# Value products of three attention stages with v as the stationary operand, two heads on the array's column halves, and a softmax normalised ahead of its transposes

## The chip, the cores and the metric

The kernel runs on one NeuronCore of a Trainium2 chip. The metric is the device time of one execution in microseconds (us), from runs of the whole program. The engines that matter here are TensorE (PE: matmuls and, as a kind of matmul, 128x128 transposes; its weight loads are a row of their own, PEld), VectorE (DVE), ScalarE (ACT) and the DMA queues. A matmul has a stationary operand, which is loaded into the array as weights, and a moving one, which streams past it; the result lands in one of eight PSUM banks.

## The reference, cut to what matters

The program is a small transformer of two layers on 256 latent and 256 context tokens, followed by a second network of four blocks. Three of its mixers contain the attention that the change touches: neighbourhood attention (8 heads of 64, 256 latent queries over 256 latent and 256 context keys, and the context's own attention), window attention (8 query heads on 2 key heads, 256 queries over 512 keys, with a sink in the sum), and a dilated attention of the second network (8 heads, 256 queries, three causal key patterns side by side). Each of them is, per head:

```
s = q @ k.T * scale + bias or mask
p = exp(s - max(s)) / (sum(exp(s - max(s))) [+ exp(sink - max(s))])
o = p @ v
```

and the heads' outputs, merged, go through an output projection. A fourth, the differential attention, uses the same step order but is not touched.

## The kernel before

All large matmuls are f32 split into a high and a low part (three products each, `mm3`, lines 211 to 214); attention's own products are plain f32. Weights stream in by DMA, ACT makes the high part and DVE the low part (`halves`, lines 258 to 266), and PE multiplies them in blocks (`block`, line 404).

Attention runs as a side stream. A `Side` (line 75) holds generators, and at the middle and the end of every projection block `tick` lets them take some steps (rate 0.6 to 1.5 steps a tick), so that attention's instructions are written between the projection's. Within an engine the build's scheduler then orders instructions by that order and by what is ready in its own model; on the chip every engine takes its queue in order.

`attend` (lines 628 to 643) is the step order of one group of units. A unit is one head and one query tile of 128 rows. In step i the scores of units i and i+1 are issued as a pair (the two heads sit on the array's row halves, lines 634 to 637), unit i gets its maximum (DVE) and exponential (ACT, with the row's sum), unit i-2 is transposed (`transposed`, lines 645 to 651: PE transposes into a bank `pT`, ACT copies it to `pTs`), and unit i-3 takes its value products (`pv`). There the transposed probabilities are the stationary operand and v moves, 64 columns of one head:

```
for j in range(4):
    net.mm(o, u.pT[:, j], u.g.v[:, j, u.h * 64:(u.h + 1) * 64], j == 0, j == 3)
```

So the output `o` (PSUM tile `oat`, in window attention `oc`) has tokens on partitions. When a group's units are through, DVE takes the reciprocal of the sums (`rden`, `crd`) and multiplies the output out of PSUM (`yna`, `yc`), PE transposes it to features on partitions (`ynt`, `yct`), and ACT and DVE split it into the operand of the output projection.

- Neighbourhood attention: classes `Lat` and `Ctx` (lines 784 to 834) and `Group.run` (lines 852 to 878), four groups f of four `Lat` units and two `Ctx` units (each `Ctx` unit covers both query tiles of the context). Beside it run the projections, the gated convolutions (`gcu`) and a second side stream, modulation sums on DVE (`aacc`, line 566).
- Window attention: class `Swa` and `swa_run` (lines 1205 to 1257), two query tiles of eight heads; heads h and h+4 are a pair. Beside it run the projections of the differential attention.
- Dilated attention: `Unit` and `Group` (lines 2073 to 2137), four groups of two heads; units with the second query tile have six key tiles, those with the first have three. The last group's steps run in `att.drain()` (line 2167), after the last projection.

## Time and profile before

| | |
|---|---|
| median of 3 runs | 2496.32 us (2495.28 to 2497.0) |
| the profiled execution: its own time / its span | 2498.09 us / 2496.3 us |
| granted TensorE clock, mean | 0.984 of full |
| busy: PE, PEld, DVE, ACT | 95%, 79%, 73%, 52% of the span |
| HBM | 181 GB/s over the span |

The span is the time from the first to the last instruction; the execution's own time also has what lies around it. Busy times are unions of an engine's records. Matmuls are pipelined, so their records overlap and a start-to-start distance tells more than a duration.

### The profile page before, as it was taken

How to read it: one execution, taken by the hardware profiler on the slowest of the kernel's cores; microseconds unless marked ns; L12 is line 12 of the kernel's file. 1: busy time of each engine (PE TensorE's matmuls, PEld its weight loads, DVE VectorE, ACT ScalarE, POOL GpSimd, SP SyncE). 2: the span in 40 equal slices, each digit the busy share in tenths (PEclk: the TensorE clock that was granted, in tenths of full speed). 3: DMA queues.
4: the chain of work that ended last, by engine and by line, in shares of the span. 5: the costliest groups of instructions: out<-in, count | busy, mean ns of one | idle time of the engine just before them, and what ended most of it. 6: DMA issues, size and time to landing. Idle time of an engine off the chain costs nothing.

```text
span 2496.3 us, 32333 instructions
## 1 busy us (share of the span) xinstructions
PE 2383.6 (95%) x11882; PEld 1981.9 (79%) x11882; DVE 1812.5 (73%) x3515; ACT 1299.0 (52%) x2230; POOL 13.0 (1%) x27
## 2 busy tenths in 40 slices
PE   7999999999899879999999999989999999999998
PEld 5878888888788658787877887877788788898886
DVE  5798988676686778989988556998744754646644
ACT  4445333232454568777776445775644544655533
POOL 0000000000000000000000000000000000000000
PEclk9999999999998999999999999999999999999999
DMA  8344455654221159999997654333665555554561
GB/s 275 115 133 163 152 186 190 215 163 166 75 81 56 55 170 321 331 324 338 313 352 264 194 189 144 102 102 126 220 199 172 186 185 167 146 153 136 191 196 51
DMA packets 381471, 455.15 MB, mean 182 GB/s; under 512 B 16680, under 2 KB 313337, under 8 KB 381305
## 3 DMA queue, kind: packets, MB, share of 16 engines
q1 hardware_dynamic: 375481, 445.86, 55.1%
q10 hardware_dynamic: 5824, 7.15, 0.9%
q8 instruction: 95, 1.56, 0.3%
q14 instruction: 71, 0.58, 0.1%
HBM read 451.91 MB, written 1.05 MB: 181 GB/s over the span
## 4 chain that ended last, share of the span: by engine, by line
PE 51%; DVE 7%; ACT 2%; DMA 2%; issue 1%; DVEq 0%; SPq 0%; ACTq 0%
PE gu L206 26%; PE acc L206 13%; PE pj L206 6%; DVE wl L226 3%; DMA wxr<-in_moe_w_dram 1%; DVE hcv L1730 1%; PE ht L209 1%; PE cvq L206 1%; PE po L206 1%; ACT wh L225 1%; PE oat L206 1%; DVE wxl L226 0%; PE mgp L206 0%; DVE c L1861 0%; PE pT L209 0%
## 5 line engine op out<-in xcount | busy, mean ns | idle before, releaser
L226 DVE TENSOR_TENSOR wl<-wr,wh 128x1024 fp32r<-128x1024 f32 (+1 forms) x510 | 590.9, 1186 | 168.7 <-ACT wh L225 167.7
L225 ACT ACTIVATE wh<-wr 128x1024 fp32r<-128x1024 f32 (+1 forms) x510 | 503.3, 1025 | 284.2 <-PE gu L206 55.9
L226 DVE TENSOR_TENSOR wl<-wxr,wh 128x1024 fp32r<-128x1024 f32 (+1 forms) x122 | 144.2, 1207 | 49.6 <-ACT wh L225 44.9
L566 DVE SCALAR_TENSOR_TENSOR aacc<-wr,sc,aacc 128x512 f32<-128x512 f32 x224 | 162.0, 761 | 14.6 <-DMA wr<-in_ada_w_dram 13.6
L206 PE MATMUL gu<-wh,xh 128*128 128x512 f32 x416 | 163.8, 394 | 2.6 <-ACT xh L229 2.6
L206 PE MATMUL gu<-wh,xl 128*128 128x512 f32 x416 | 162.9, 392 | 0.7 <-DVE xl L230 0.7
L206 PE MATMUL gu<-wl,xh 128*128 128x512 f32 x416 | 162.5, 391 | 0.0
L206 PE MATMUL gu<-wl,mgh 128*128 128x512 f32 (+1 forms) x384 | 146.3, 381 | 8.1 <-DVE wl L226 8.1
L225 ACT ACTIVATE wh<-wxr 128x1024 fp32r<-128x1024 f32 (+1 forms) x122 | 123.7, 1043 | 54.2 <-PE acc L206 13.9
L206 PE MATMUL gu<-wh,mgh 128*128 128x512 f32 (+1 forms) x384 | 144.9, 377 | 1.3 <-ACT wh L225 1.2
L226 DVE TENSOR_TENSOR wxl<-wr,wxh 128x1024 fp32r<-128x1024 f32 (+1 forms) x94 | 110.0, 1182 | 46.8 <-ACT wxh L225 43.7
L206 PE MATMUL gu<-wh,mgl 128*128 128x512 f32 (+1 forms) x384 | 143.1, 373 | 0.6 <-DVE mgl L226 0.6
L206 PE MATMUL acc<-wh,hid 128*128 128x512 f32 x416 | 135.3, 396 | 0.0
L435 ACT ACTIVATE sg<-gu,ry 128x256 f32<-128x256 f32 x88 | 41.2, 472 | 164.0 <-PE gu L206 158.8
L225 ACT ACTIVATE wxh<-wr 128x1024 fp32r<-128x1024 f32 (+1 forms) x94 | 95.0, 1024 | 43.4 <-PE acc L206 20.2
L436 DVE SCALAR_TENSOR_TENSOR sg<-gu,ry,sg 128x256 f32<-128x256 f32 x88 | 42.0, 480 | 103.8 <-ACT sg L435 103.8
L206 PE MATMUL acc<-wh,hh 128*128 128x512 f32 x352 | 115.9, 399 | 1.1 <-ACT wh L225 1.1
L206 PE MATMUL gu<-wxh,xh 128*128 128x512 f32 x288 | 113.6, 395 | 1.7 <-ACT xh L229 1.6
L206 PE MATMUL gu<-wxh,xl 128*128 128x512 f32 x288 | 113.2, 393 | 1.4 <-DVE ri L286 0.8
L206 PE MATMUL gu<-wxl,xh 128*128 128x512 f32 x288 | 113.0, 392 | 0.0
L206 PE MATMUL pj<-wh,xh 128*128 128x512 f32 (+1 forms) x248 | 96.9, 392 | 0.6 <-ACT xh L229 0.6
L206 PEld LDWEIGHTS gu<-wh,xh 128*128 128x128 f32 x416 | 78.3, 188 | 20.5 <-ACT xh L229 4.7
(548 smaller groups left out, 5847.0 us busy)
## 6 DMA issues: line engine op xcount, KB each, us to landing
wr<-in_ffn_w_dram SPq DMA_DIRECT2D x176, 512.0 KB
wr<-in_moe_w_dram SPq DMA_DIRECT2D x124, 512.0 KB
wr<-in_ffn_w_dram SPq DMA_DIRECT2D x45, 1024.0 KB
wr<-in_ada_w_dram SPq DMA_DIRECT2D x42, 1024.0 KB
wr<-in_moe_w_dram SPq DMA_DIRECT2D x28, 1024.0 KB
wxr<-in_ffn_w_dram SPq DMA_DIRECT2D x44, 512.0 KB
wxr<-in_moe_w_dram SPq DMA_DIRECT2D x40, 512.0 KB
wr<-in_attn_w_qkv_dram SPq DMA_DIRECT2D x54, 256.0 KB
```

The costliest lines, as they stand in the source:

```text
L206: self.nc.tensor.matmul(out, lhsT, rhs, start=start, stop=stop)
L209: self.nc.tensor.transpose(out, in_, self.ident)
L225: self.nc.scalar.activation(h, src, AF.Copy)
L226: self.split_op = self.nc.vector.tensor_sub(l, src, h.bitcast(F32))
L435: nc.scalar.activation(g, p[:, 0:n], AF.Silu, scale=rs[tt])
L436: nc.vector.scalar_tensor_tensor(g, p[:, n:2 * n], rs[tt], g, op0=OP.mult, op1=OP.mult)
L566: self.nc.vector.scalar_tensor_tensor(a[:, s], w, col, a[:, s], op0=OP.mult, op1=OP.add)
L1730: V.scalar_tensor_tensor(a, xx[:, j:j + 256], tap(j), a, op0=OP.mult, op1=OP.add)
```

## The change

The value products swap their operands: v, 64 columns of one head, becomes the stationary operand and the transposed probabilities move, 128 columns. The output has features on partitions: head h lands on PSUM partitions 64h to 64h+63 (in window attention the key head decides, h // 4), so two heads fill the two column halves of the array and their products are issued in turns, as a pair, in the step of the odd unit (`pvs`). The output is then split straight out of PSUM; the multiplication by the reciprocal and the transposes of the output are gone, and the deferred step that held them (`att.post`) too. Since rows of the output are now features, the normalisation cannot be done there: each unit divides its exponentials by their sum ahead of its transposes (`norm` and `normed`, one step after the exponential), by a reciprocal on DVE and a scaling in place, on ACT in neighbourhood attention and on DVE in the other two. In window attention the output's features come in another order, and the rows of `od_w_out` are permuted on the host to match.

```diff
--- before.py
+++ after.py
@@ attend
                 units[i].s()
+            if 0 < i <= n and hasattr(units[i - 1], "pvs"):
+                units[i - 1].norm()
             if 0 <= i - lag < n:
                 units[i - lag].t()
-            if 0 <= i - lag - 1 < n:
-                units[i - lag - 1].pv()
+            j = i - lag - 1
+            if 0 <= j < n:
+                if not hasattr(units[j], "pvs"):
+                    units[j].pv()
+                elif j % 2:
+                    for ab in zip(units[j - 1].pvs(), units[j].pvs()):
+                        for f in ab:
+                            f()
             yield
+
+    def normed(self, e, den, n=1, act=False):
+
+        rd = self.sm(n, "rd")
+        self.nc.vector.reciprocal(rd, den)
+        w = e.shape[1] // n
+        for j in range(n):
+            x, r = e[:, j * w:(j + 1) * w], rd[:, j:j + 1]
+            if act:
+                self.copy(x, x, r)
+            else:
+                self.nc.vector.tensor_scalar(x, x, r, None, op0=OP.mult)
 
     def transposed(self, e, nkt):
         p = self.ps([128, nkt, 128], "pT")
@@ -798,15 +820,19 @@
                                        OP.add, OP.max, mx[:, 1:2])
                 V.tensor_scalar(mx[:, 1:2], mx[:, 1:2], -1.0, None, op0=OP.mult)
                 u.e = net.t2([128, 512], "pe")
-                nc.scalar.activation(u.e, s, AF.Exp, bias=mx[:, 1:2], accum_out=u.g.den[:, u.qt, u.h:u.h + 1])
+                u.den = net.sm(1, "den")
+                nc.scalar.activation(u.e, s, AF.Exp, bias=mx[:, 1:2], accum_out=u.den)
+
+            def norm(u):
+                net.normed(u.e, u.den, act=True)
 
             def t(u):
                 u.pT = net.transposed(u.e, 4)
 
-            def pv(u):
-                o = u.g.out()[:, u.qt, u.h]
-                for j in range(4):
-                    net.mm(o, u.pT[:, j], u.g.v[:, j, u.h * 64:(u.h + 1) * 64], j == 0, j == 3)
+            def pvs(u):
+                hs = slice(64 * u.h, 64 * u.h + 64)
+                o = u.g.out()[hs, u.qt * 128:(u.qt + 1) * 128]
+                return [lambda j=j: net.mm(o, u.g.v[:, j, hs], u.pT[:, j], j == 0, j == 3) for j in range(4)]
 
         class Ctx(Lat):
             def mms(u):
@@ -823,15 +849,18 @@
                 mx = net.sm(2, "mx")
                 V.tensor_reduce(mx, s, AX.X, OP.max, negate=True)
                 u.e = net.t2([128, 512], "pe")
+                u.den = net.sm(2, "den")
                 for j in range(2):
                     nc.scalar.activation(u.e[:, j * 256:(j + 1) * 256], s[:, j], AF.Exp, bias=mx[:, j:j + 1],
-                                         accum_out=u.g.den[:, 2 + j, u.h:u.h + 1])
-
-            def pv(u):
-                for j in range(2):
-                    o = u.g.out()[:, 2 + j, u.h]
-                    for i in range(2):
-                        net.mm(o, u.pT[:, 2 * j + i], u.g.v[:, 2 + i, u.h * 64:(u.h + 1) * 64], i == 0, i == 1)
+                                         accum_out=u.den[:, j:j + 1])
+
+            def norm(u):
+                net.normed(u.e, u.den, 2, act=True)
+
+            def pvs(u):
+                hs = slice(64 * u.h, 64 * u.h + 64)
+                return [lambda j=j, i=i: net.mm(u.g.out()[hs, (2 + j) * 128:(3 + j) * 128], u.g.v[:, 2 + i, hs],
+                                                u.pT[:, 2 * j + i], i == 0, i == 1) for j in range(2) for i in range(2)]
 
         vall = self.a8([128, 4, 512], F32, "v")
 
@@ -846,13 +875,12 @@
 
             def out(g):
                 if g.o is None:
-                    g.o = net.ps([128, 4, 2, 64], "oat")
+                    g.o = net.ps([128, 512], "oat")
                 return g.o
 
             def run(g):
                 f = g.f
                 g.bias = net.t4([128, 2, 2, 256], "bias")
-                g.den = net.sm(8, "den").rearrange("p (a b) -> p a b", a=4)
                 for qt in range(2):
                     for i in range(2):
                         rq = qt * 2 + i
@@ -863,18 +891,7 @@
                 nc.gpsimd.tensor_add(b, b, cmask.to_broadcast([128, 16, 64]))
                 units = [Lat(g, h, qt) for qt in range(2) for h in range(2)] + [Ctx(g, h, 2) for h in range(2)]
                 yield from net.attend(units)
-                rd = net.sm(8, "rden")
-                V.reciprocal(rd, g.den.rearrange("p a b -> p (a b)"))
-                y = net.t2([128, 8, 64], "yna")
-                V.tensor_mul(y, g.o.rearrange("p a h d -> p (a h) d"), rd[:, :, None].to_broadcast([128, 8, 64]))
-
-                def turn():
-                    tp = net.ps([128, 4, 128], "ynt")
-                    for qt in range(4):
-                        net.tr(tp[:, qt], y[:, 2 * qt:2 * qt + 2, :])
-                    net.split(yT[1][0][:, f], yT[1][1][:, f], tp.rearrange("p a b -> p (a b)"))
-
-                att.post(2, turn)
+                net.split(yT[1][0][:, f], yT[1][1][:, f], g.o)
                 yield
 
         for f in range(4):
@@ -1225,13 +1242,15 @@
                 nc.scalar.activation(mx[:, 2:3], sink[:, h:h + 1], AF.Exp, bias=mx[:, 0:1])
                 V.tensor_add(u.den[:, h:h + 1], u.den[:, h:h + 1], mx[:, 2:3])
 
+            def norm(u):
+                net.normed(u.e, u.den[:, u.h:u.h + 1])
+
             def t(u):
                 u.pT = net.transposed(u.e, 4)
 
-            def pv(u):
-                g = u.h // 4
-                for j in range(4):
-                    net.mm(u.o[0][:, u.h], u.pT[:, j], cv[:, j, g * 64:(g + 1) * 64], j == 0, j == 3)
+            def pvs(u):
+                gs = slice(64 * (u.h // 4), 64 * (u.h // 4) + 64)
+                return [lambda j=j: net.mm(u.o[0][gs, u.h % 4], cv[:, j, gs], u.pT[:, j], j == 0, j == 3) for j in range(4)]
 
         def swa_run(qt):
             qs = slice(qt * 128, qt * 128 + 128)
@@ -1239,21 +1258,10 @@
             us = [Swa(o, den, h + 4 * i, qt) for h in range(4) for i in range(2)]
             for i, _ in enumerate(self.attend(us)):
                 if i == 1:
-                    o[0] = self.ps([128, 8, 64], "oc")
+                    o[0] = self.ps([128, 4, 128], "oc")
                 yield
-            rd = self.sm(8, "crd")
-            V.reciprocal(rd, den)
-            y = self.t2([128, 8, 64], "yc")
-            V.tensor_mul(y, o[0], rd[:, :, None].to_broadcast([128, 8, 64]))
-
-            def turn():
-                tp = self.ps([128, 4, 128], "yct")
-                for f in range(4):
-                    self.tr(tp[:, f], y[:, 2 * f:2 * f + 2])
-                self.split(yT[0][:, 0:4, qs], yT[1][:, 0:4, qs], tp)
-                self.ready.add(("swa", qt))
-
-            att.post(2, turn)
+            self.split(yT[0][:, 0:4, qs], yT[1][:, 0:4, qs], o[0])
+            self.ready.add(("swa", qt))
             yield
 
         class Diff:
@@ -2097,18 +2105,21 @@
                     c = slice(gs[0] * n, (gs[-1] + 1) * n)
                     V.scalar_tensor_tensor(e[:, c], dl[:, off + c.start:off + c.stop], slope, s, op0=OP.mult, op1=OP.add)
                 V.tensor_reduce(mx, e[:, 0:3 * n], AX.X, OP.max, negate=True)
-                nc.scalar.activation(e[:, 0:3 * n], e[:, 0:3 * n], AF.Exp, bias=mx, accum_out=g.den[:, 2 * qt + h:2 * qt + h + 1])
+                u.den = net.sm(1, "den")
+                nc.scalar.activation(e[:, 0:3 * n], e[:, 0:3 * n], AF.Exp, bias=mx, accum_out=u.den)
+
+            def norm(u):
+                net.normed(u.e[:, 0:384 * (u.qt + 1)], u.den)
 
             def t(u):
                 nt = 3 * (u.qt + 1)
                 u.pT = [net.transposed(u.e[:, j * 128:min(j + 4, nt) * 128], min(4, nt - j)) for j in range(0, nt, 4)]
 
-            def pv(u):
-                g, h, qt = u.g, u.h, u.qt
-                nt = 3 * (qt + 1)
-                for j in range(nt):
-                    b, kt = j // (qt + 1), j % (qt + 1)
-                    net.mm(g.out()[:, qt, h], u.pT[j // 4][:, j % 4], g.v[:, kt, b, h * 64:(h + 1) * 64], j == 0, j == nt - 1)
+            def pvs(u):
+                g, qt = u.g, u.qt
+                nt, hs = 3 * (qt + 1), slice(64 * u.h, 64 * u.h + 64)
+                return [lambda j=j: net.mm(g.out()[hs, qt * 128:(qt + 1) * 128], g.v[:, j % (qt + 1), j // (qt + 1), hs],
+                                           u.pT[j // 4][:, j % 4], j == 0, j == nt - 1) for j in range(nt)]
 
         class Group:
             def __init__(g, f):
@@ -2119,21 +2130,12 @@
 
             def out(g):
                 if g.o is None:
-                    g.o = net.ps([128, 2, 2, 64], "oat")
+                    g.o = net.ps([128, 256], "oat")
                 return g.o
 
             def run(g):
-                g.den = net.sm(4, "den")
                 yield from net.attend([Unit(g, h, qt) for qt in (1, 0) for h in range(2)])
-                rd = net.sm(4, "rden")
-                V.reciprocal(rd, g.den)
-                y = net.t2([128, 4, 64], "yna")
-                V.tensor_mul(y, g.o.rearrange("p a h d -> p (a h) d"), rd[:, :, None].to_broadcast([128, 4, 64]))
-                yield
-                tp = net.ps([128, 256], "ynt")
-                for qt in range(2):
-                    net.tr(tp[:, qt * 128:(qt + 1) * 128], y[:, 2 * qt:2 * qt + 2, :])
-                net.split(yT[0][:, g.f], yT[1][:, g.f], tp)
+                net.split(yT[0][:, g.f], yT[1][:, g.f], g.o)
                 yield
 
         att = Side(1.2)
@@ -2219,7 +2221,11 @@
     rel = np.clip(col[None, :] - col[:, None] + 15, 0, 30)
     consts["k_rpb"] = np.asarray(inputs["ev_rpb"])[0][:, 4:11][:, :, rel].transpose(0, 2, 1, 3)
     for name in [n for n in _INS if n != "ev_rpb"] + list(consts):
-        a = np.ascontiguousarray(inputs[name] if name in inputs else consts[name])
+        a = inputs[name] if name in inputs else consts[name]
+        if name == "od_w_out":
+            a = np.array(a)
+            a[0, 0:512] = a[0, 0:512].reshape(2, 4, 64, 1024).transpose(1, 0, 2, 3).reshape(512, 1024)
+        a = np.ascontiguousarray(a)
         arrays[f"in_{name}_dram"] = a
         args[name] = nc.dram_tensor(f"in_{name}_dram", a.shape, mybir.dt.from_np(a.dtype), kind="ExternalInput").ap()
     out = nc.dram_tensor("out_0_dram", (1, 256, 1024), F32, kind="ExternalOutput").ap()
```

## Rows read from the trace of the kernel before

**Rows 1.** Page: busy time, share of the span, instructions of each engine.

```profile
PE 2383.6 (95%) x11882; PEld 1981.9 (79%) x11882; DVE 1812.5 (73%) x3515; ACT 1299.0 (52%) x2230; POOL 13.0 (1%) x27
```

**Rows 2.** Stretches: length, busy PE, PEld, DVE, ACT, POOL; clock; DMA.

```profile
96.00:285.00 189.00, 186.53 (x1068) 158.78 (x1067) 166.65 (x375) 78.88 (x178) 5.20 (x2) 1.00 0.48 151
713.00:802.00 89.00, 85.73 (x518) 72.84 (x518) 56.68 (x247) 40.63 (x108) 0.00 (x0) 0.90 0.16 51
2165.00:2287.00 122.00, 118.50 (x800) 112.69 (x799) 65.19 (x91) 71.68 (x132) 0.00 (x0) 0.99 0.50 154
2273.00:2287.00 14.00, 10.63 (x84) 9.68 (x83) 9.42 (x15) 8.77 (x19) 0.00 (x0) 0.88 0.51 174
```

**Rows 3.** Tile pTs, its matmuls: count, ns min/median/max, first and last start, form.

```profile
L206 PE MATMUL oat<-v,pTs x192: 217/275/323, 99.8 to 230.8; 128*128 128x64 f32 x192
...
L206 PE MATMUL oat<-dvv,pTs x144: 217/275/421, 2178.8 to 2285.6; 128*128 128x64 f32 x144
...
L206 PE MATMUL oc<-swa,pTs x128: 218/275/422, 724.5 to 792.7; 128*128 128x64 f32 x128
```

**Rows 4.** Timeline of PE around one unit's value products: start, us, instruction, count.

```profile
99.60 0.33 PE L206 MATMUL pj<-wl,a_1h 128*128 128x384 f32 x1
99.77 1.00 PE L206 MATMUL oat<-v,pTs 128*128 128x64 f32 x8
100.58 0.42 PE L206 MATMUL pj<-wh,a_1l 128*128 128x384 f32 x1
100.84 0.33 PE L206 MATMUL pj<-wh,a_1h 128*128 128x384 f32 x1
```

**Rows 5.** Timeline of PE and its weight loads: matmuls on 32-column tiles.

```profile
25.62 0.15 PEld L206 LDWEIGHTS ada<-adw,scw 128*32 128x32 f32 x6 [0.17 <-issue]
25.63 1.06 PE L206 MATMUL ada<-adw,scw 128*32 128x512 f32 x6
```

**Rows 6.** Timeline of PE around two bursts of paired scores, dilated attention.

```profile
2168.35 0.34 PE L206 MATMUL pj<-wxh,xl 128*128 128x384 f32 x1
2168.62 1.57 PE L206 MATMUL S<-dqk 64*128 64x256 f32 x12
2170.11 0.45 PE L206 MATMUL pj<-wxh,xh 128*128 128x384 f32 x1
2170.40 0.34 PE L206 MATMUL pj<-wxl,xh 128*128 128x384 f32 x1
...
2174.50 0.94 PE L206 MATMUL S<-dqk 64*128 64x128 f32 x12
2175.37 0.88 PE L209 MATMUL pT<-cm,de 128*128 128x128 f32 x6
2176.00 0.42 PE L206 MATMUL pj<-wxh,xh 128*128 128x384 f32 x1
```

**Rows 7.** Tile yna: the multiplications of the output out of PSUM.

```profile
L869 DVE TENSOR_TENSOR yna<-oat,rden x4: 691/692/692, 127.5 to 231.1; 128x512 f32<-128x512 f32 x4
L2131 DVE TENSOR_TENSOR yna<-oat,rden x4: 423/424/425, 2188.8 to 2286.0; 128x256 f32<-128x256 f32 x4
```

**Rows 8.** Groups of DVE, differential attention: busy us, mean ns | idle before.

```profile
L1277 DVE TENSOR_SCALAR pe<-pe,drd 128x512 f32<-128x512 f32 x8 | 3.9, 483 | 0.2
...
L1275 DVE RECIPROCAL drd<-dden 128x2 f32<-128x2 f32 x8 | 1.3, 160 | 2.2 <-ACT pe L1272 2.1
```

**Rows 9.** Groups of ACT: a copy with one scale per partition.

```profile
L222 ACT ACTIVATE dvv<-pj,ry 128x384 f32<-128x384 f32 x8 | 4.3, 574 | 3.1 <-PE pj L206 3.1
```

**Rows 10.** Waits of ACT, 96 to 242 us: total, times, longest.

```profile
ACT pe L801 <- DVE mx L799: 20.0, 11, 6.3
```

**Rows 11.** Timeline of PE, window attention: scores of a pair, then of single heads.

```profile
720.38 1.13 PE L206 MATMUL S<-swa 64*128 64x512 f32 x4
...
747.80 1.12 PE L206 MATMUL S<-swa 64*128 64x512 f32 x2
...
750.78 1.12 PE L206 MATMUL S<-swa 64*128 64x512 f32 x2
```

**Rows 12.** The stretch from 771 to 787 us, columns as in rows 2.

```profile
771.00:787.00 16.00, 14.47 (x70) 12.94 (x69) 7.84 (x46) 5.26 (x15) 0.00 (x0) 0.57 0.10 38
```

## Prediction

> **What bounds the kernel now.** I read the page first: PE is busy 95% of the span and DVE 73% [rows 1]. A matmul's record overlaps the next one's, so this share alone proves little; the second view is the busy time by stage, over the three stretches in which the changed code runs [rows 2]. Neighbourhood attention and the projection behind it (96 to 285 us) have PE busy 186.53 of 189.00 us, and DVE 166.65. Window attention (713 to 802) has PE 85.73 of 89.00, DVE 56.68. Dilated attention (2165 to 2287) has PE 118.50 of 122.00, DVE 65.19, ACT 71.68. So in all three the matmul queue is the nearest bound: a PE step saved is time saved, as long as the engine that feeds it keeps up. In the third stage that is easy, in the second likely, in the first doubtful: DVE is idle there only 189.0 - 166.7 = 22.3 us. The one stretch where PE really stands still is the tail of the dilated stage, after its last projection (2273 to 2287, PE 10.63 of 14.00 us): there the attention chain itself sets the end.
>
> **Value products.** Today one unit (a head and a query tile) issues 4, 6 or 3 f32 products. The trace has two MATMULs for each: 192 + 144 + 128 = 464 of them, every one behind a weight load of 128 columns, with only 64 columns moving [rows 3]. A unit of four runs from 99.77 to 100.58, 0.81 us for 8 MATMULs, and the matmul behind it takes 0.26 instead of 0.17 to hand over [rows 4]: 0.90 us a unit, 1.80 a pair, 0.1125 a MATMUL. A pair of units with six products is 24 x 0.1125 = 2.70, with three 1.35.
>
> Afterwards v stands still (64 columns of weights) and 128 columns of probabilities move, two heads on two column halves. The trace has no 128x64 tile, so I bound it by its two nearest rows. Column tiles do run side by side: six MATMULs on 32-column tiles with 512 columns moving, two rounds of three (of four in the code; a record can be missing), take 1.06 us in all [rows 5]. And two heads on row halves with exactly 128 columns moving run 12 MATMULs, six rounds, from 2174.50 to 2175.37, 0.87 us [rows 6]. Against the same burst with 256 columns (2168.62 to 2170.11, 1.49) the difference is 0.62 / 6 = 0.103 us a round; 0.87 - 6 x 0.103 = 0.25 is the cost of changing the array's mode at the start, and the matmul after the long burst needs 0.29 instead of 0.17. With 0.27 instead of 0.17 ahead of the burst that makes some 0.45 a burst for loads of 128 columns. By 0.103 us per 128 columns the two rounds of 512 on column tiles are 0.82, six in turn would be 2.5; a last record reaches 0.19 beyond its successor's start (1.00 against 0.81, [rows 4]), so of the 1.06 next to nothing is left inside, and for 32 columns I put 0.2 for entry and exit. For 64 columns I take 0.38, nearer to the burst of scores, whose rounds are the same. A pair of four products is then 8 x 0.103 + 0.38 = 1.20 us (1.02 to 1.27) against 1.80; of six 1.62 against 2.70; of three 1.00 against 1.35.
>
> Sum on PE: 12 pairs in the first stage and 8 in the second, 20 x 0.60 = 12.0; 4 x (1.08 + 0.35) = 5.7 in the third. **Transposes of the output** go: 16 + 8 + 8, at 0.63 / 6 = 0.105 each [rows 6], 3.4. Together 21.1 us of PE: 8.9 in the first stage, 5.6 in the second, 6.6 in the third.
>
> **Normalisation.** What goes: ten multiplications out of PSUM, 0.69 us or 0.42 [rows 7], and ten reciprocals. What comes, once a unit, 56 times, between the exponential and the transposes: a reciprocal on DVE (0.16) and a scaling (0.48 for 512 columns on DVE, [rows 8]). In the first stage the scaling is ACT's: 24 units, 16 of 512 columns and 8 of two times 256. A copy of 384 columns with a scale per partition takes 0.574 [rows 9], stretched to 512 columns 0.77, to 256 0.38: 16 x 0.77 + 16 x 0.38 = 18.4 us more on ACT, which works 78.88 of the 189.00 us there. DVE there: 24 x 0.16 - 4 x (0.69 + 0.16) = +0.4, nothing. In the second, DVE: 16 x (0.16 + 0.48) - 2 x 0.85 = +8.5 on 56.7 of 89; in the third 8 x (0.16 + 0.72) + 8 x (0.16 + 0.36) - 4 x 0.58 = +9.0 on 65.2 of 122 (0.72 and 0.36 are 0.483 stretched to 768 and 384 columns). None of that fills an engine; what counts is its place. The unit's transposes now wait for one more step. What hides it is that a unit's transposes come two steps of the planner after its scores, with projection matmuls in between; without that cover it costs 0.65 to 0.9 us a unit. The first stage's scaling also queues in ACT, where the weight splits and the copies of transposed probabilities stand behind it, and its reciprocal queues behind DVE's modulation sums: there ACT already waits 20.0 us, 11 times, for DVE's maxima [rows 10].
>
> **What of it reaches the end.** First stage: 8.9, but DVE keeps its load, and PE cannot run ahead of the weight splits; I take 60%, 5.3 (0 if DVE becomes the bound, 8.9 if not). Second: 60% of 5.6, 3.4, since PE is not full there now and DVE gets 8.5 more. Third: three of four groups lie under projections, 3 x 1.64 = 4.9, of which 4.3. The fourth is bare: its chain loses the multiplication and two transposes (0.42 + 0.21) and 1.4 of value products, and gains the hop of 0.9 at its start and DVE's queue for the next units; I call it 0, between -1.5 and +1.5. Against this: the two heads of a pair must be ready together. For the scores, which are paired already, it mostly holds, but in the second stage two of eight pairs came apart: one head alone needs 1.12 us for its two MATMULs, where both heads need 1.13 for four [rows 11]. A value pair that comes apart costs 1.20 more than one that holds (a second burst with its mode change). Four of 28 would cost 4.8, of which 3.3 on the path. Sum: 5.3 + 3.4 + 4.3 + 0 - 3.3 = 9.7 us.
>
> **The clock** is a term without a sign. From 771 to 787 us the granted clock is 0.57 of full [rows 12], that is mostly the lower of the two levels, 1.2 GHz, with PE busy 14.47 of 16 us. It costs some 16 x 0.43 = 6.9 us. If the new bursts do without it, that much comes on top; a second such episode takes as much. I take 0 and keep both ends.
>
> **A page that speaks against it.** In the row on column tiles the second round's weight loads are out 0.15 us after the first's, while the first round still runs, and all of it ends after 1.06 [rows 5]. The Trainium skill, TensorE: Matmul & The Clock Gate, section Part 3: Packing small matmuls (The mechanism), says that a weight load overlaps matmuls in flight only where their row groups differ; two column halves share all rows. By that rule the next loads would stand bare between the rounds, which is rival 1 and its time. The row contradicts it, for 32 columns.
>
> **Rivals.** (1) Loads bare between the rounds: 20 x 8 + 4 x 12 + 4 x 6 = 232 rounds, each with some 0.09 (what stands ahead of a burst of scores for its first loads, [rows 6]): 21 us, all of the gain, 2496. Against it: [rows 5]. (2) Pairs come apart for the most part, because the odd head's copy arrives later than the even one's: with half of them 16.8 of the 21.1 are gone and the time is 2496; with all 28, 20 x 1.20 + 4 x 1.62 + 4 x 1.00 = 34.5, net 13 slower, 2510. (3) The other side: **the normalising hop sits on the path of the transposes**. Place: ACT's queue in the first stage (behind a reciprocal that waits in DVE's), DVE's in the other two. Price: PE waits up to 0.65 to 0.9 us in a unit that no projection fills. It decides from 13.0 / 56 = 0.23 us a unit on, the gain on the path ahead of what pairs lose; at 0.9 in half the units, 25 us, the time is 12 higher, 2508. For it: [rows 10], and PE takes its queue in order. Against it: PE is full in these stretches because other matmuls fill such waits already. (4) DVE becomes the bound in the first stage and the second gives half: 4.3 + 1.7 - 1.5 = 4.5, 2492. (5) All of it reaches the end, 21.1, and the clock's 6.9: 2468.
>
> **How the numbers follow.** The profiled execution has a span of 2496.3 and its own time is 2498.1; the median of the runs is 2496.3, 0.07% lower, so the sum is taken off the median: 2496.3 - 9.7 = 2486.6. Chances: forecast (2478 to 2492) 0.60; rival 1 0.04; rival 2 0.10; rival 3 0.12; rival 4 0.10; rival 5 0.04. The range reaches to 2473 below and 2500 above; outside lie most of rivals 3 and 5 and the worst of 2. A measurement of this kernel tells some 0.2%, 5 us, from no change. Faster by more: 0.57 of the forecast, rival 5, half of 4 and a little of 2, 0.70. Within: the rest of these, rival 1 and half of rival 2, 0.16. Slower: rival 3 and the worst of 2, 0.14.
>
> **What the profile after would show.** Value products with the form 128x64 tiles and 128 columns moving, two at a time, 16 in about 1.0 us: the pair holds; bursts of 8 at 0.11 each: it came apart. The matmuls after a burst handing over in 0.29: the mode change. PE waiting for the scaled probabilities ahead of the transposes by more than a few us in a stage: rival 3. The stage from 96 to 285 as long as before with DVE at 95%: rival 4. The tail from 2273 to 2287 longer or shorter than 13.7 us tells the bare chain. The forecast is wrong above all if the weight splits on DVE, not PE, set the pace of the first stage, or if the planner's new order opens a gap that drops the clock elsewhere.

## The result, and the profile after

The changed kernel is slower: 2511.17 us median (2509.77 to 2514.74, four runs) against 2496.03 (2495.28 to 2497.0, four runs of before beside them). The ratio is 1.0052, with an interval of 1.0036 to 1.0068. The prediction said 2486.6, within 2473 to 2500, so both its sign and its range were wrong. The profiled execution has a span of 2508.0.

The first view is the page's busy time of after, whole span:

```profile
PE 2372.8 (95%) x11850; PEld 1958.4 (78%) x11850; DVE 1825.5 (73%) x3583; ACT 1316.7 (53%) x2262; POOL 12.9 (1%) x27
```

PE is busy 10.8 us less than in [rows 1] and the program takes 11.7 us longer. So PE stands still for longer. The 10.8 is about half of the 21.1 that the prediction takes away; part of the rest hides in matmuls that take longer at a lower clock (the run without the division, below, has PE busy 2367.7 us, 15.9 less than before, at a mean granted clock of 0.983). Where PE stands still is in the windows. The stages now lie elsewhere in time, so I cut them at their own ends, rounded to whole us: neighbourhood attention from its first transposed probabilities to the last `gcu` product, dilated attention from its first scores to the output projection (118.0 us before and 122.0 after, unrounded). First before, then after (window, its length, busy time and number of records of each engine, granted clock, DMA share, GB/s):

```profile
95.00:240.00 145.00, 142.53 (x869) 122.47 (x867) 125.00 (x289) 66.03 (x154) 5.20 (x2) 1.00 0.46 146
2169.00:2287.00 118.00, 114.50 (x778) 108.97 (x775) 62.35 (x88) 68.20 (x127) 0.00 (x0) 0.99 0.51 156
```

```profile
95.00:251.00 156.00, 140.59 (x851) 113.33 (x851) 129.52 (x315) 82.64 (x187) 5.04 (x2) 0.96 0.44 135
2176.00:2297.00 121.00, 111.91 (x754) 102.38 (x752) 67.99 (x112) 68.05 (x125) 0.00 (x0) 0.96 0.48 143
```

The neighbourhood stage went from 145 to 156 us. PE's idle time in it rose from 145.00 - 142.53 = 2.5 to 156.00 - 140.59 = 15.4, and the granted clock fell from 1.00 to 0.96. DVE has 129.52 of 156 us: it is not the bound. What PE waits for is in the view of waits. Each line names who waited, for what, us in total, how often, the longest. After, 90 to 252 us, and then 2157 to 2298:

```profile
PE pT L209 <- ACT pe L222: 15.4, 7, 4.0
...
PE pT L209 <- DVE rd L658: 8.5, 3, 4.7
PE pT L209 <- DVE de L665: 0.6, 1, 0.6
```

In the same two stretches before, PE waited ahead of `pT` for 0.4 and for 2.9 us. So what PE idles in the first stage is nearly all transposes that wait for the scaling on ACT, and 9.1 us in the third are transposes that wait for the scaling on DVE (the view names the reciprocal where that one ended last; in the longest of these waits, the unit's scaling ends at 2291.90 us, within 0.1 us of the reciprocal named). This is the prediction's rival 3.

One such wait in full, after, from the timeline (start, length, engine, line, operation, tiles; in brackets the idle time before it and what ended it):

```profile
143.35 0.96 PE L206 MATMUL S<-qk 64*128 64x512 f32 x6
...
144.54 0.69 ACT L824 ACTIVATE pe<-S,mx 128x512 f32<-128x512 f32 x1 [1.94 <-DVE mx L821]
145.07 0.41 DVE L818 TENSOR_REDUCE mx<-S 128x1 f32<-128x256 f32 x1
...
145.40 0.48 DVE L564 TENSOR_SCALAR aacc<-wr,sc 128x512 f32<-128x512 f32 x1
145.80 0.48 DVE L819 CUSTOM_DVE_ANT_0 S<-S,bias,mx 128x256 f32<-128x256 f32 x1
...
146.20 0.48 DVE L564 TENSOR_SCALAR aacc<-wr,sc 128x512 f32<-128x512 f32 x1
146.60 0.14 DVE L821 TENSOR_SCALAR mx<-mx 128x1 f32<-128x1 f32 x1
146.66 0.74 DVE L566 SCALAR_TENSOR_TENSOR aacc<-wr,sc,aacc 128x512 f32<-128x512 f32 x1
146.84 0.69 ACT L824 ACTIVATE pe<-S,mx 128x512 f32<-128x512 f32 x1 [1.03 <-DVE mx L821]
147.32 0.15 DVE L658 RECIPROCAL rd<-den 128x1 f32<-128x1 f32 x1
...
147.52 0.71 ACT L222 ACTIVATE pe<-pe,rd 128x512 f32<-128x512 f32 x1
...
148.29 0.48 PE L209 MATMUL pT<-cm,pe 128*128 128x128 f32 x1 [3.98 <-ACT pe L222]
```

The unit's exponential ends at 145.23. Its reciprocal, 0.15 us of work, starts at 147.32: ahead of it in DVE's queue stand the next unit's maximum (four instructions between 145.07 and 146.74) and three instructions of the modulation sums (0.48, 0.48 and 0.74 us), one behind the other with no idle time. Its scaling starts at 147.52: ahead of it in ACT's queue stands the next unit's exponential, which itself waits 1.03 us for that maximum. The hop is 0.15 + 0.71 us of work and takes 3.0 us. PE has nothing else in its queue that it may do first and stands still for 3.98 us.

The value products came out as priced. After, timeline of PE, a pair of four products and, from the dilated tail, a pair of six:

```profile
107.91 1.09 PE L206 MATMUL oat<-pTs,v 128*64 128x128 f32 x16
108.93 0.66 PE L209 MATMUL qkt<-cm,qkn 128*128 128x128 f32 x4
...
2295.16 1.53 PE L206 MATMUL oat<-pTs,dvv 128*64 128x128 f32 x24
2296.62 0.55 PE L209 MATMUL pT<-cm,de 128*128 128x128 f32 x3
```

From the burst's start to the next instruction it is 1.02 us for four products of two heads and 1.46 for six.

### The profile page after: what moved, and what is told of

It reads as the page before. It is cut to its first block, busy times and chain, and to the rows that moved or that the text cites. A ratio compares the mean times of both kernels' runs of the same rounds, so it can differ in the third digit from the quotient of the medians.

```text
span 2508.0 us, 32382 instructions
## 1 busy us (share of the span) xinstructions
PE 2372.8 (95%) x11850; PEld 1958.4 (78%) x11850; DVE 1825.5 (73%) x3583; ACT 1316.7 (53%) x2262; POOL 12.9 (1%) x27
## 4 chain that ended last, share of the span: by engine, by line
PE 50%; DVE 8%; ACT 2%; DMA 1%; issue 1%; SPq 0%; DVEq 0%; ACTq 0%
PE gu L206 26%; PE acc L206 13%; PE pj L206 5%; DVE wl L226 3%; DVE hcv L1738 1%; PE ht L209 1%; PE po L206 1%; PE cvq L206 1%; DMA wr<-in_moe_w_dram 1%; ACT wh L225 1%; DVE wxl L226 1%; PE oat L206 0%; PE mgp L206 0%; DVE c L1869 0%; PE pT L209 0%
## 5 line engine op out<-in xcount | busy, mean ns | idle before, releaser
L226 DVE TENSOR_TENSOR wl<-wr,wh 128x1024 fp32r<-128x1024 f32 (+1 forms) x510 | 591.2, 1187 | 165.6 <-ACT wh L225 159.5
L566 DVE SCALAR_TENSOR_TENSOR aacc<-wr,sc,aacc 128x512 f32<-128x512 f32 x224 | 161.3, 754 | 17.5 <-DMA wr<-in_ada_w_dram 16.5
```

Source lines behind the costliest of these rows:

```text
L226: self.split_op = self.nc.vector.tensor_sub(l, src, h.bitcast(F32))
L566: self.nc.vector.scalar_tensor_tensor(a[:, s], w, col, a[:, s], op0=OP.mult, op1=OP.add)
```

## Experiments

Each run is compared with runs of the kernel before on the same chip, whose medians were 2496.4 to 2497.8. The intervals reach 2 to 5 us to either side, and between two runs the difference of the medians and that of the ratios can differ by up to 4 us; a difference of a few us between two versions is not told. Theory A is rival 3, the hop on the transposes' path; theory B says that the paired value products don't pay.

**The division left out.**

```diff
-            if 0 < i <= n and hasattr(units[i - 1], "pvs"):
-                units[i - 1].norm()
```

> The changed kernel with the division left out (its exponentials go to the transposes unscaled; neither the reciprocal nor the scaling is issued), everything else of the change kept: value products in pairs, no transposes of the output. Theory A (the normalising hop stands on the path of the transposes, and PE's queue waits there): the value products' gain shows at last, 2496 less 10 to 20 us, 2476 to 2486, and PE no longer waits ahead of pT for a scaling. Theory B (paired value products don't save: pairs that come apart, mode changes): little changes against the kernel after, 2505 to 2512. Theory C (half and half): 2488 to 2503.

Measured 2481.74, ratio 0.9931 (0.9914 to 0.9949). Without the hop the value products are worth 16 us, and the hop costs the changed kernel 2511.2 - 2481.7 = 29 us. The wait and the window of the first stage:

```profile
PE pT L209 <- ACT pe L822: 1.7, 3, 1.1
```

```profile
95.00:235.00 140.00, 137.91 (x858) 110.53 (x855) 124.38 (x291) 66.61 (x157) 5.58 (x2) 1.00 0.48 151
```

PE is full again, at a clock of 1.00. Theory B falls. The run leaves out the hop's work together with its place in the queues; which of the two counts is asked further down.

**The hop alone, on the kernel before.**

```diff
+            if 0 < i <= n and hasattr(units[i - 1], "norm"):
+                units[i - 1].norm()
...
-                V.tensor_mul(y, g.o.rearrange("p a h d -> p (a h) d"), rd[:, :, None].to_broadcast([128, 8, 64]))
+                V.tensor_copy(y, g.o.rearrange("p a h d -> p (a h) d"))
```

> The kernel before with one part of the change alone: each unit's exponentials are divided by their sum one step behind the exponential, and the output is copied out of PSUM where it was multiplied. Value products, their operands and the output's transposes are as before. Theory A (hop): slower than before by as much as the change lost plus what its value products gained, 2496 + 15 + 10 to 20 = 2515 to 2530. Theory B (paired value products are at fault): 2494 to 2500.

Measured 2515.91, ratio 1.0070 (1.0052 to 1.0088): 18 us slower with the old value products. So the hop costs by itself, and 11 us more when the value products are paired. In the first stage of its trace PE waits less than half as long for the scaling as in the changed kernel (6.6 us, 3 times, against 15.4, 7 times). By its trace the neighbourhood stage is 154.1 us long, 9.1 longer than before, where the changed kernel's is 17.0 longer than that of the run without the division. Why the waits are shorter beside the old value products I did not trace. And part of its 18 us is the clock's: the mean granted clock of its runs is 0.979 against 0.984 before, an estimated 13 us.

**One more step of lag.** Scores and transposes of a unit lie three steps apart, in all three stages; then the same lag in the kernel before, and with the division left out.

```diff
         n = len(units)
+        lag = lag or (3 if hasattr(units[0], "pvs") else 2)
         for i in range(n + lag + 1):
```

> The changed kernel with one more step between a unit's scores and its transposes in the three stages (lag 3 where it was 2). Theory A (the hop has too little cover): most of the wait ahead of the transposes goes, 2485 to 2497. If buffers (an exponential or a score held one step longer, in pools of 8) are short, part of it comes back as waits for them, 2500 to 2510. Theory B: no change, 2507 to 2513. The bare tail of the dilated stage grows by at most a step in each theory, 1 to 2 us.

Measured 2490.83, ratio 0.9975 (0.9963 to 0.9986): 20 us less than with lag 2, and faster than before.

> The kernel before with the one more step of lag in the three stages, nothing else: the control to the changed kernel with that lag. Theory A (the lag gave its 20 us there because it covers the normalising hop, which the kernel before doesn't have): 2493 to 2501, no gain. Rival (the lag itself helps whatever is in the unit, so the changed kernel's gain under it is not the hop's): 2484 to 2491.

Measured 2511.98, ratio 1.0072 (1.0054 to 1.0089). On the kernel before the step costs 16 us, so its gain on the changed kernel is not a gain of the order as such; it is cover for the hop. That it would cost so much I had not expected. Most of it goes with the clock: the mean granted clock of its runs is 0.980 against 0.985 before, an estimated 11 of the 16 us. In its trace the dilated stage alone goes from 118 to 124 us, 3.9 of these 6 in the tail behind the last projection, where the clock is 0.51 over 14 us. Why this order lowers the clock stays open.

> The changed kernel with lag 3 in the three stages and the division left out. Theory A, with the hop covered by the third step: what is left of it is the distance to the run with lag 3 and the division, 2491; fully covered, 2487 to 2493; half covered, 2478 to 2484 (the changed kernel without the division and with lag 2 ran 2482).

Measured 2486.12, ratio 0.9958 (0.9944 to 0.9972). Under lag 3 the hop costs 2490.8 - 2486.1 = 4.7 us, where it cost 29 under lag 2; the two intervals overlap, so these 4.7 are not told from nothing.

**The lag where it pays.** In the traces the window stage was longer with lag 3 than with lag 2, so this version has lag 3 in the neighbourhood and dilated attention only.

```diff
-                yield from net.attend(units)
+                yield from net.attend(units, 3)
...
-                yield from net.attend([Unit(g, h, qt) for qt in (1, 0) for h in range(2)])
+                yield from net.attend([Unit(g, h, qt) for qt in (1, 0) for h in range(2)], 3)
```

> The changed kernel with lag 3 in the neighbourhood and the dilated attention, lag 2 in window attention, where the trace with lag 3 showed the stage 4 to 8 us longer than with lag 2. If stages add up: 2491 less 4 to 8, 2483 to 2487. If the window stage's length is an episode of the clock that falls where it falls: 2488 to 2494.

Measured 2488.17, ratio 0.9972 (0.9959 to 0.9985). It beats both kernels; from lag 3 everywhere it can't be told. The time lies at the lower end of the range for a window stage whose length is an episode of the clock, 1 us above the range for stages that add up, so it doesn't decide between them. Its first stage, waits and window:

```profile
PE pT L209 <- ACT pe L222: 4.6, 3, 2.9
```

```profile
97.00:238.00 141.00, 135.93 (x827) 108.80 (x825) 120.46 (x294) 76.26 (x175) 4.80 (x2) 0.99 0.49 150
```

The wait is 4.6 us where it was 15.4, and the stage takes 141 us where it took 156.

**Stage by stage.** The change in one stage alone, the other two as before.

> The change in the neighbourhood attention alone, the other two stages as before. In the trace of after this stage ended 11 us later than in that of before; with stages that add up the kernel is slower than before by that, 2505 to 2510. If the loss there is made by something that the other stages' edits share (the sums' tiles, the planner's order as a whole): 2496 to 2502.

Measured 2508.45, ratio 1.0051 (1.0033 to 1.0070): 12 us slower, as expected if stages add up.

> The change in window attention alone; neighbourhood and dilated attention as before. If stages add up as their ends in the two traces stand (the stage ended 4.2 us nearer to the kernel before than it began), 2492, with some 2 us either way: faster than before. If the gain there was only that of an episode at the lower clock that moved by chance, it is 2496 give or take 5 and the clock of 771 to 787 us tells.

Measured 2497.06, ratio 0.9995 (0.9983 to 1.0006): no change, as if the gain that I had read from the two traces in this stage were the clock's.

> The change in the dilated attention alone. Theory A (hop on the path there too, as the waits of 8.5 us ahead of its transposes in the trace of after say): 2499 to 2504. Rival (the stage's loss in the trace of after is the clock's episode, which fell longer there by chance, and the value products' gain and the hop cancel): 2493 to 2498.

Measured 2500.44, ratio 1.0013 (0.9999 to 1.0026), not told from no change. The three add up to 1.0059, the whole change is 1.0052. Nearly all of the loss is the neighbourhood attention, where both links of the hop stand in busy queues. With lag 3 in that stage alone:

> The change in the neighbourhood attention alone, with lag 3 there. Theory A: the run with lag 2 there gave 2508; with the hop covered the stage ends some 4.6 us ahead of before (145.0 to 140.4 us in the traces): 2489 to 2494. If the gain of lag 3 came from all stages alike: 2498 to 2504.

Measured 2499.15, ratio 1.0000 (0.9987 to 1.0013). The step takes 9 of that stage's 12 us of loss back. The gain of 4 to 9 us below the kernel before that I expected is not there: the time lies in the range of the rival, by which the gain of lag 3 comes from all stages alike. Its trace has the gain where theory A puts it, 140.5 us for the stage where before has 145.0. It loses that in the tail of the dilated stage, whose code is that of before: from the last projection to the output projection 17.6 us, before 13.7. The granted clock of the dilated stage is 0.95 over 122 us, 6.1 us of lost clock, where before has 0.99 over 118, 1.2 us. The two stages, in the columns of the windows above:

```profile
95.00:236.00 141.00, 135.62 (x828) 108.95 (x826) 121.59 (x298) 76.67 (x174) 4.75 (x2) 0.99 0.49 150
2162.00:2284.00 122.00, 118.50 (x778) 112.84 (x777) 62.92 (x89) 68.74 (x127) 0.00 (x0) 0.95 0.51 158
```

The mean clock of its runs, 0.982 against 0.984, says that the profiled execution is no exception. So this run alone does not decide between the two.

**Which link of the hop.** Lag 2 again, the changed kernel with the reciprocal on GpSimd (as a power of -1), and with the first stage's scaling on DVE.

```diff
-        self.nc.vector.reciprocal(rd, den)
+        self.nc.gpsimd.tensor_tensor(rd, den, self.neg1.to_broadcast([128, n]), op=OP.pow)
```

> The changed kernel (lag 2) with the reciprocal of each unit's sum on GpSimd, which has almost nothing to do, in place of DVE (a pool of small tiles gives up one of its 20 buffers for the constant it needs). Theory A1 (the price of the hop is the place in DVE's queue: in the trace of after the reciprocal starts 0.1 to 8.8 us behind the exponential's end in the neighbourhood attention, and PE waited 15.4 us there): most of the wait goes, 2490 to 2500. Theory A2 (the price is the scaling itself and its place in ACT's queue, or that the transposes stand too early in PE's): 2505 to 2513.

Measured 2503.97, ratio 1.0029 (1.0017 to 1.0041): 7 of the hop's 29 us are gone (6 by the ratios). Its timeline at the same unit as above:

```profile
141.16 0.69 ACT L826 ACTIVATE pe<-S,mx 128x512 f32<-128x512 f32 x1 [1.94 <-DVE mx L823]
...
142.02 0.56 POOL L660 TENSOR_TENSOR rd<-den,neg 128x1 f32<-128x1 f32 x1 [27.64 <-ACT pe L826]
...
143.45 0.69 ACT L826 ACTIVATE pe<-S,mx 128x512 f32<-128x512 f32 x1 [1.02 <-DVE mx L823]
...
144.13 0.71 ACT L222 ACTIVATE pe<-pe,rd 128x512 f32<-128x512 f32 x1
...
144.89 0.47 PE L209 MATMUL pT<-cm,pe 128*128 128x128 f32 x1 [4.03 <-ACT pe L222]
```

The reciprocal is there at 142.58, and the scaling still starts at 144.13, since the next unit's exponential is ahead of it on ACT. PE waits 4.03 us, as before. At this unit, one freed queue of two is of no use.

```diff
-                net.normed(u.e, u.den, act=True)
+                net.normed(u.e, u.den)
```

> The changed kernel (lag 2) with the scaling of the neighbourhood attention on DVE, behind its reciprocal, where it was ACT's; so ACT's link is out of the hop and DVE's stays, with 24 x 0.48 = 11.5 us more work for DVE. Theory A1: the wait ahead of the transposes stays, 2508 to 2518. Theory A2 with ACT's queue as its place: 2493 to 2502.

Measured 2512.67, ratio 1.0061 (1.0047 to 1.0074), as with the scaling on ACT. Here both instructions stand in DVE's queue, in program order behind the next unit's maximum, and in the first stage of its trace PE waits 16.5 us for them ahead of `pT`.

**The place in the step.** Lag 2, the normalisation issued ahead of the next unit's scores, maximum and exponential; then directly behind the unit's own exponential.

```diff
+            if 0 < i <= n and hasattr(units[i - 1], "pvs"):
+                units[i - 1].norm()
             if i < n:
...
                 units[i].s()
-            if 0 < i <= n and hasattr(units[i - 1], "pvs"):
-                units[i - 1].norm()
```

> The changed kernel (lag 2) with a unit's normalisation issued ahead of the next unit's scores, maximum and exponential in the step, where it was behind them. Theory A3 (the hop's price is its place: reciprocal and scaling stand behind the next unit's maximum and exponential in two in-order queues): the waits ahead of the transposes fall from 15 us to about 5 in the neighbourhood attention, 2488 to 2498. Theory A4 (the price is the three links of the hop themselves, wherever they stand): 2506 to 2513.

Measured 2501.22, ratio 1.0020 (1.0011 to 1.0030); its wait in the first stage:

```profile
PE pT L209 <- ACT pe L222: 6.8, 4, 3.1
```

> The changed kernel (lag 2) with a unit's normalisation issued in its own step, directly behind its exponential. Theory A3: as with the normalisation ahead of the next unit's scores, 2486 to 2498; if DVE and ACT then stand still for the links of one unit in turn, the next unit's maximum comes late and part is given back, 2498 to 2506. Theory A4: 2506 to 2513.

Measured 2498.57, ratio 1.0006 (0.9994 to 1.0017). Same engines, same lag, same three links: the order within the step alone takes 10 and 13 us of the 29 away (8 and 11 by the ratios), and more than half of the first stage's wait (7.2 us are left in the second run). So theory A4, by which only the length of the links counts, falls, and the place behind the next unit is shown for that part. But A3 expected more: the first run is 3 us above its range, the second at its upper end. The rest of the price stays until the lag is longer, and how it splits between the links' own length and their place is not shown.

**What didn't add up.** With lag 3 in two stages, these edits gain nothing more:

> Lag 3 in the neighbourhood and dilated attention and the normalisation ahead of the next unit's scores. Theory A3: the rest of the hop's price under that lag, some 5 us of 2488, goes in part, 2482 to 2487. If the order under the longer lag is no longer what makes it late: 2486 to 2491.

Measured 2494.42, ratio 0.9990 (0.9979 to 1.0001).

> Lag 3 in the neighbourhood and dilated attention and the normalisation directly behind the unit's own exponential. Theory A3: 2481 to 2487; if the order no longer matters under the longer lag, 2486 to 2491.

Measured 2493.70, ratio 0.9992 (0.9983 to 1.0001).

> Lag 3 in the neighbourhood and dilated attention, as in the run of that name, and the reciprocal on GpSimd. If both covers add up: the 2488 of that run less what is left of the hop there, some 5, 2481 to 2486. If the clock's episodes decide what is left: 2485 to 2492.

Measured 2495.93, ratio 0.9989 (0.9979 to 0.9999). All three miss every range that I gave. By their medians they lie 5 to 8 us above the version without them (2488.17), by their ratios 4 to 5, and each interval just overlaps that version's: that nothing is gained is shown, that something is lost is likely and not shown. A scaling that comes earlier may no longer be needed earlier; that would explain a gain of nothing. For a loss there are candidates (the power takes 0.55 to 1.75 us where DVE's reciprocal takes 0.15, and the build writes another order for each), but no run that tells.

**The worth of the pair.** Lag 3 in two stages, the two heads' products one head after the other.

```diff
-                    for ab in zip(units[j - 1].pvs(), units[j].pvs()):
-                        for f in ab:
-                            f()
+                    for u in (units[j - 1], units[j]):
+                        for f in u.pvs():
+                            f()
```

> Lag 3 in the neighbourhood and dilated attention, and the two heads of a pair issue their value products one head after the other where they took turns, same operands, same count, same places in the order. Theory A (rounds of two heads run side by side, 0.103 us each): 8 rounds become 16 in a pair of four, 20 x 0.82 + 4 x 1.24 + 4 x 0.62 = 23.8 us more on PE, of which most reaches the end: 2505 to 2513. Rival (loads stand bare between the rounds anyway, or the heads don't overlap): 2486 to 2492.

Measured 2498.93, ratio 1.0006 (0.9997 to 1.0015): 11 us slower than in turns (8 by the ratios), so the pairing pays. The timeline of PE shows what one head alone costs:

```profile
119.48 1.09 PE L206 MATMUL oat<-pTs,v 128*64 128x128 f32 x8
120.50 0.44 PE L206 MATMUL pj<-wh,a_0h 128*128 128x384 f32 x1
```

Eight MATMULs of one head take 1.02 us, as long as the sixteen of a pair: the two column halves do run side by side. It cost less than the 24 us I expected, in part because the build let the heads of many pairs overlap where one ends and the other begins; a burst at 109.63 us has all 16 MATMULs of a pair and takes 1.51 us, not two times 1.02.

## Why the prediction was wrong, point by point

**What bounds the kernel: right, but read too kindly.** PE was the bound, and each saved step was time saved as long as the engine that feeds it kept up: the run without the division has PE busy 15.9 us less and is 16.0 us faster. I then judged "keeps up" by DVE's and ACT's idle time in the stage. DVE never became the bound (rival 4: 129.52 of 156 us), nor ACT (82.64). It was not the amount of their work that counted but its order.

**Value products: right in price.** Priced 1.20 us a pair of four, with 0.1 and 0.1 of it in the neighbours. Measured 1.02, after an entry of 0.27 (0.17 without a change of mode) and with 0.11 more for the matmul behind it, so 1.2; of six 1.46 and the same, 1.7 (priced 1.62). Rival 1, bare loads between the rounds, falls: a round of two heads takes 0.109 us. The Trainium skill, TensorE: Matmul & The Clock Gate, section Part 3: Packing small matmuls (The mechanism), lists that a weight load overlaps matmuls in flight only where row groups differ, though its first paragraph also lets a load into the background weight buffer go ahead. The trace does not agree with the list for two column halves of 64: both share all rows, and at 0.109 us a round no load shows.

**Pairs that come apart: right in size by luck, wrong in kind.** I took 4 of 28 pairs that come apart in whole, 4.8 us on PE and 3.3 of it on the path. None did. But in 9 of 28 the build set the even head's first product alone ahead of the rest. After, timeline of PE, such a pair of four:

```profile
171.36 0.43 PE L206 MATMUL oat<-pTs,v 128*64 128x128 f32 x2
171.72 0.50 PE L206 MATMUL gcu<-a_0h,wh 128*128 128x512 f32 x1
...
172.62 1.09 PE L206 MATMUL oat<-pTs,v 128*64 128x128 f32 x14
173.63 0.50 PE L206 MATMUL gcu<-a_0h,wh 128*128 128x512 f32 x1
```

The product alone takes 0.36 us, and the fourteen MATMULs that are left still take 1.01, as the sixteen of a whole pair do. With the second change of mode, 0.1 us on either side, I estimate 0.55 us a pair, 5 us for the nine. That is about the size of what PE's busy time lacks in the run without the division, 15.9 us in place of 21.1.

**What of the gain reaches the end: put too low, and the stages agree only in part.** The sum without the hop was 5.3 + 3.4 + 4.3 - 3.3 = 9.7. The run without the division is 16.0 faster than before. By the two traces it ended the neighbourhood stage 5.6 us earlier, gained 7.2 in the window stage and 2.6 in the dilated one, up to the transposes behind the output projection. The second is too good by a part that is the clock's: that stage has 0.93 over 160 us before (some 11 us lost) and 0.94 over 152 in this run (some 9).

**The normalising hop: the step that failed.** The prediction says that it is hidden "with projection matmuls in between", at most 0.65 to 0.9 us a unit bare, and that "PE is full in these stretches because other matmuls fill such waits already". Both are wrong. PE's queue is in order, so the projection matmuls that stand behind a waiting transpose don't fill its wait; those ahead of it are cover, and that was enough for the exponential (0.4 us of waits before) and not for a step behind it. And the price isn't the 0.15 + 0.71 us of its two instructions. It is in good part the place: written behind the next unit's maximum and exponential, in two in-order queues, in DVE's with modulation sums between, the hop lasts until these are done, and that was 3.0 us in the unit shown. In the program it takes one of the two steps of lag between scores and transposes. I had named both queues and who stands in them, modulation sums included, [rows 10], and then priced the hop by its own instructions. Measured, it is 29 us, 0.53 a unit on average, over the 0.23 from which rival 3 decides. Rival 3 named the right place and its 2508 is near 2511, but its price is right by luck: it had 0.9 us in half of the units, and the trace has ten long waits, seven in the first stage and three in the third, of up to 4.7 us, with the lower clock beside them. The Trainium skill, PSUM — Partial Sum Buffer, section Engine vs sequencer instructions, says that the queues of ScalarE and VectorE are strictly first in, first out, and that MATMULs start in program order. The timeline above agrees: the reciprocal starts 2.09 us behind its exponential's end, the scaling right behind the other unit's exponential, and PE starts nothing for 3.98 us.

**The bare tail: right.** I had 0, give or take 1.5. From the last projection to the output projection it took 12.64 us (2284.82 to 2297.46), where before took 13.74. But these don't compare: after, the output projection starts with other groups' rows while the last group's products are still to come.

```profile
2284.82 0.34 PE L206 MATMUL pj<-wh,xl 128*128 128x384 f32 x1
...
2292.05 3.19 PE L209 MATMUL pT<-cm,de 128*128 128x128 f32 x15 [4.72 <-DVE rd L658]
...
2297.46 0.50 PE L206 MATMUL po<-wh,ydh 128*128 128x512 f32 x1
...
2299.51 0.76 PE L206 MATMUL oat<-pTs,dvv 128*64 128x128 f32 x9
```

Up to the transposes behind the output projection it is 24.71 us after and 24.74 before. The wait of 4.72 us, 1.86 longer than the one before, is paid for by shorter products and by this overlap.

**The clock: taken as 0, and it wasn't.** With the longer waits of PE come stretches at the lower of the two levels, 1.2 GHz. In the first stage there was none before and there are four after, 3.4 us each, from 117.1, 147.9, 161.5 and 199.1 us; each begins within 0.6 us of the end of a wait of 2.1 to 4.0 us ahead of `pT`. At 0.96 of 156 us that is 6.2 us, so part of the hop's 29 are the clock's. The two traces, after and without the division, bear this out: of 26.1 us between their spans, 13.7 are longer waits ahead of `pT` in the first stage (15.4 against 1.7) and 5.8 in the third (9.1 against 3.3). The mean granted clocks, 0.981 and 0.983, make some 5 us of the rest. Over all runs the clock's part is larger, 0.979 after and 0.984 without the division: an estimated 13 of the 29 us (both are estimates from rounded clocks). I have no run that has the waits without the clock's drop, so what the waits would cost at the full clock is not shown.

## What to carry to other kernels

When a step is put between two engines' work, price it by what stands ahead of it in each in-order queue on its way, not by its own duration; here that was the neighbour unit's work, which waits itself, and the sums of another stream. If the consumer's queue is in order, work behind the consumer fills no wait: give the new step its own step of lag, or put it ahead of the next unit's work in the program. In this kernel the lag gave more (20 us against 10 and 13), and both together no more than the lag alone. A control, the same lag without the step, tells cover from a better order.

## What the runs showed of the hardware that I had not expected

The same wait can be followed by a short or a long stretch at the lower clock. The dilated tail has the same code in the kernel before and in the run with the change in the first stage alone. In both PE waits 2.86 us for an exponential ahead of `pT`. Before, and then that run (timeline of PE, and windows of some 14 and 17 us from the wait on):

```profile
2278.25 2.87 PE L209 MATMUL pT<-cm,de 128*128 128x128 f32 x12 [2.86 <-ACT de L2100]
...
2277.00:2291.00 14.00, 12.23 (x75) 11.08 (x76) 6.20 (x12) 6.81 (x17) 0.00 (x0) 0.88 0.54 198
```

```profile
2287.11 0.87 PE L209 MATMUL pT<-cm,de 128*128 128x128 f32 x6 [2.86 <-ACT de L2117]
...
2286.00:2303.00 17.00, 14.91 (x66) 13.76 (x67) 5.91 (x10) 6.12 (x15) 0.00 (x0) 0.60 0.46 159
```

The clock is 0.88 over 14 us in one and 0.60 over 17 in the other, 1.7 against 6.8 us of lost clock, and the output projection begins 8.4 us behind the wait's end in one, 12.3 in the other. So 4 us of difference between single traces in this stage say nothing of the change. Nor do they in the window stage, where the clock cost 6.9 us before [rows 12] and 3.4 after (7 us at 0.51):

```profile
786.00:793.00 7.00, 5.70 (x32) 5.37 (x33) 4.38 (x21) 3.85 (x11) 0.00 (x0) 0.51 0.01 1
```

From the last `cqt` transpose to the last `po` product that stage took 159.5 us before and 155.6 after, but 155.6 also in the run with the change in the first stage alone, where its code is that of before; and the run with the change in this stage alone gave 0.9995.
